# A third seven-product pair, wider operations and alternating PSUM banks in a decoder block's up/gate product

## The chip, the cores and the metric

The kernel runs on 1 core of a Trainium2 chip. The metric is the device time of one execution in microseconds (us). The five engines of the core are called here TensorE (PE in the profile; its weight loads are PEld), VectorE (DVE), ScalarE (ACT), GpSimd (POOL) and SyncE (SP, which issues nearly all DMA transfers here). Matmul results go to PSUM, which has eight banks of 512 float32 columns; everything else lies in SBUF.

## The reference

One decoder block on 256 rows of width 2048, in float32: two attention mixers, a gated sum, LayerNorm, a SwiGLU layer and LayerNorm again. The part that matters here is the SwiGLU layer, whose hidden width is 5632:

```python
def _swiglu(h, w_ffn_in, w_ffn_out):
    g, u = jnp.split(h @ w_ffn_in, 2, axis=-1)
    return (jax.nn.silu(g) * u) @ w_ffn_out
```

`h` is 256 x 2048, `w_ffn_in` 2048 x 11264 and `w_ffn_out` 5632 x 2048.

## The kernel before

Every product is computed to nearly float32 with the fp32r matmul: a value is split into a high part (ScalarE casts it, L71) and a low part (VectorE subtracts the high part, L72), and each product is three matmuls, high x high, high x low and low x high (`mm3`, L91 to L93). A matmul takes a 128 x 128 stationary tile of activations and a 128 x 512 moving tile of weights.

The hidden width is cut into 11 blocks of 512 columns. Block 0 is a plain product. Blocks 1 to 10 run through `pair_product` (L708). Such a block has four results, gate and up for the two halves of the rows (c11, c12, c21, c22: `acc_fg0`, `acc_fu0`, `acc_fg1`, `acc_fu1`), each in a PSUM bank of the tag `acc`. It takes the 16 slices of the inner dimension two at a time: eight pairs, each with one load of 1 MB (four tiles of 512 columns, `raw_fp`). An ordinary pair needs eight products, 24 matmuls. Pairs 2 and 4 (the third and the fifth) of blocks 1 to 9 use a Strassen-like form with seven products, 21 matmuls: VectorE combines the four weight tiles with four adds and subtractions of 512 columns (L737 to L740, in place in `raw_fp`), and ScalarE and VectorE split these combined tiles again. Four of the seven products (p1, p6, p7, p5) are shared among results; they add up over the seven-product pairs of a block in four banks of the tag `tmp`, and VectorE adds them into the results afterwards (L752 to L755, then L758 to L761). Matching forms of the activations are made once, in `row_forms` (L676), during block 0.

The splits work on halves of a load: 1024 columns, or 512 where only three tiles are needed. Names: `whfp_5g` is the high part of pair 5's gate half, `wlfp_5g` the low part, `whfp_4t` and `wlfp_4t` those of pair 4's combined tiles (t2, t3). High and low parts lie in two rings of eight buffers, the loads in a ring of three. After the results come silu and product (L774, L775, L787), a transpose of 32 x 32 blocks on VectorE (L264) into `rt`, and eight ticks later 16 transfers of 32 KB that SyncE issues (L286), which put `rt` into place in `act`.

The kernel is written in a tile framework whose list scheduler sets each engine's order at compile time, from the program's order and its own estimates; every engine then runs its instructions strictly in that order. The order in this part is thus not written by hand, and a change of sizes or buffers can move instructions.

Of the kernel before, what the change touches and what calls it, by code (L numbers as in the profile page):

```python
# [12 lines left out]
F32R = mybir.dt.float32r  # L13
# [4 lines left out]
P = 128  # L18
# [11 lines left out]
N = 512  # L30
# [14 lines left out]
def decoder_block(ctx, tc, xT, x, wz, lam_qk, subln, wa, wb, wo, g1, b1, b1T, wf, wfp, wfo, g2, b2,  # L45
# [9 lines left out]
    def bigt(shape, dt, name):  # L55
        return big.tile([P] + shape, dt, tag="big", name=name)
# [7 lines left out]
    def acc(name):  # L64
        return ps.tile([P, N], F32, tag="acc", name=name)

    def tmp(name):
        return ps.tile([P, N], F32, tag="tmp", name=name)

    def split(src, hi, lo, eng=None):  # L70
        nc.scalar.copy(hi, src)  # L71
        (eng or nc.vector).tensor_sub(lo, src, hi)  # L72


    def split_weights(part, name, eng=None):
        wh = wp.tile([P, 2, N], F32R, tag="wh", name="wh" + name)
        wl = wp.tile([P, 2, N], F32R, tag="wl", name="wl" + name)
        split(part.rearrange("p (a n) -> p a n", n=N), wh, wl, eng)
        return wh, wl

    def weights(src, name, loads=1, pool=()):
        raw = wp.tile([P, 2048], F32, tag="raw", name="raw_" + name, bufs=3)
# [88 lines left out]
    def weights_and_x(src, name):  # L171
        c = int(name.split("_")[-1])
        for i in range(2):
            k0 = 4 * c + 2 * i
            raw = wp.tile([P, 2, N], F32, tag="raw", name="raw%d_%s" % (i, name), bufs=3)
            sv = src[:, i * 1024:(i + 1) * 1024].rearrange("p (a n) -> p a n", n=N)
            if k0 == 0:
                wh = wp.tile([P, 2, N], F32R, tag="wh", name="whf")
                wl = wp.tile([P, 2, N], F32R, tag="wl", name="wlf")
                xss = []  # L180
                for a in range(2):
                    xss.append(x_part(a, 1))
                    nc.sync.dma_start(raw[:, a, :], sv[:, a, :])
                for a in range(2):
                    split_x(xss[a], a, 1)
                    split(raw[:, a, :], wh[:, a, :], wl[:, a, :])
                yield wh, wl
            else:
                xs = x_part(k0, 2)
                nc.sync.dma_start(raw, sv)  # L190
                split_x(xs, k0, 2)
                yield split_weights(raw.rearrange("p a n -> p (a n)"), "%d_%s" % (i, name))
# [477 lines left out]

    SEVEN = (2, 4)
    forms = []

    def row_forms():  # L676
        ns = len(SEVEN)
        full = bigt([NM, 2 * ns, P], F32, "hfull")
        fs = bigt([4, ns, P], F32, "forms")
        hl = bigt([2, 4, ns, P], F32R, "formshl")  # L680
        for m in range(NM):
            for n, i in enumerate(SEVEN):
                nc.vector.tensor_add(full[:, m, 2 * n:2 * n + 2, :], hth[m][:, 2 * i:2 * i + 2, :], htl[m][:, 2 * i:2 * i + 2, :])
        a = [[full[:, m].rearrange("p (n t) q -> p n t q", t=2)[:, :, t, :] for t in range(2)] for m in range(NM)]
        nc.vector.tensor_add(fs[:, 0], a[1][0], a[1][1])
        nc.vector.tensor_sub(fs[:, 1], fs[:, 0], a[0][0])
        nc.vector.tensor_sub(fs[:, 2], a[0][0], a[1][0])
        nc.vector.tensor_sub(fs[:, 3], a[0][1], fs[:, 1])
        split(fs, hl[:, 0], hl[:, 1])
        forms.append(hl)  # L690

    def stat_s(f, n):
        return forms[0][:, 0, f - 1, n, :], forms[0][:, 1, f - 1, n, :]

    def load_pair(j, i):
        raw = wp.tile([P, 4, N], F32, tag="raw", name="raw_fp%d_%d" % (j, i), bufs=3)
# [2 lines left out]

    def halves(src, name):  # L700
        n = src.shape[1]
        wh = wp.tile([P, 2, N], F32R, tag="wh", name="wh" + name)
        wl = wp.tile([P, 2, N], F32R, tag="wl", name="wl" + name)
        split(src, wh[:, 0:n], wl[:, 0:n])
        return [(wh[:, a, :], wl[:, a, :]) for a in range(n)]


    def pair_product(j):  # L708
        nk = KD // 2
        seven = SEVEN if j < NB_F - 1 else ()  # L710
        c11, c12, c21, c22 = [acc("acc_f%s_%d" % (c, j)) for c in ("g0", "u0", "g1", "u1")]
        ps_ = {}
        for i in range(nk):
            nm = "fp%d_%d" % (j, i)
            raw = load_pair(j, i)
            k0, k1 = 2 * i, 2 * i + 1
            first, final = i == 0, i == nk - 1
            if i not in seven:
                b11, b21 = halves(raw[:, 0:2], nm + "g")
                b22, b12 = halves(raw[:, 2:4], nm + "u")  # L720
                for ac, m, w0, w1 in ((c11, 0, b11, b21), (c12, 0, b12, b22), (c21, 1, b11, b21), (c22, 1, b12, b22)):
                    mm3(ac, *stat_h(m, k0), *w0, first, False)
                    mm3(ac, *stat_h(m, k1), *w1, False, final)
                tick()
                tick()
                continue
            n = seven.index(i)
            s0, s1 = n == 0, n == len(seven) - 1
            if s0:
                for f in (1, 6, 7, 5):  # L730
                    ps_[f] = tmp("p%d_%d" % (f, j))
            b11, b21 = halves(raw[:, 0:2], nm + "g")
            b22, = halves(raw[:, 2:3], nm + "u")
            mm3(ps_[1], *stat_h(0, k0), *b11, s0, s1)
            mm3(c11, *stat_h(0, k1), *b21, False, False)
            mm3(c12, *stat_s(4, n), *b22, False, False)
            nc.vector.tensor_sub(raw[:, 2], raw[:, 2], raw[:, 3])  # L737
            nc.vector.tensor_sub(raw[:, 3], raw[:, 3], raw[:, 0])
            nc.vector.tensor_add(raw[:, 0], raw[:, 2], raw[:, 0])
            nc.vector.tensor_sub(raw[:, 1], raw[:, 1], raw[:, 0])  # L740
            t2, t4 = halves(raw[:, 0:2], nm + "t2")
            t3, t1 = halves(raw[:, 2:4], nm + "t3")
            tick()
            mm3(ps_[6], *stat_s(2, n), *t2, s0, s1)
            mm3(ps_[7], *stat_s(3, n), *t3, s0, s1)
            mm3(ps_[5], *stat_s(1, n), *t1, s0, s1)
            mm3(c21, *stat_h(1, k1), *t4, False, False)
            tick()
            if s1:
                p1, u2, u3, t = [scr("%s_%d" % (c, j)) for c in ("p1", "u2", "u3", "u4")]  # L750
                nc.scalar.copy(p1, ps_[1])
                nc.vector.tensor_add(u3, p1, ps_[6])  # L752
                nc.vector.tensor_add(u2, u3, ps_[7])
                nc.vector.tensor_add(u3, u3, ps_[5])
                nc.vector.tensor_add(t, u2, ps_[5])  # L755
        if not seven:
            return (c11, c12), (c21, c22)
        nc.vector.tensor_add(p1, p1, c11)  # L758
        nc.vector.tensor_add(u3, u3, c12)
        nc.vector.tensor_add(u2, u2, c21)  # L760
        nc.vector.tensor_add(t, t, c22)  # L761
        return (p1, u3), (u2, t)
# [125 lines left out]
    with tc.manual_schedule():  # L888
# [26 lines left out]
        j = NB_D - 1  # L915
# [74 lines left out]
```

## Time and profile before

| | us |
|---|---|
| median of 3 runs | 1380.2 |
| lowest, highest | 1379.7, 1380.85 |
| profiled execution, own time | 1384.1 |
| its span in the trace | 1382.3 |
| TensorE busy in the span | 1365.0 (99%) |
| VectorE busy | 916.9 (66%) |
| ScalarE busy | 644.5 (47%) |

A share of busy time is an average over stages with different limits. What a change in one stage is worth is read from that stage: what each engine does there from one block to the next, and what ends its waits. The blocks 1 to 10 run from 705.26 to 1132.22 us of the span.

### The profile page before, as it was taken

Reading aid. Unit: us, or ns where it says so; the run is one execution under the profiler, and the core shown is the slowest. Engines: PE = TensorE matmul, PEld = TensorE weight load, DVE = VectorE, ACT = ScalarE, POOL = GpSimd, SP = SyncE. Lnnn points to the kernel's source line nnn. Section 1 sums busy time; section 2 is a strip of 40 time slices with the busy share of each in tenths; the row PEclk is TensorE's granted clock in tenths of the full one; section 3 lists DMA queues with packets and bytes.
Section 4 is the critical chain, followed back from the end, with each engine's and each line's share of the span. In section 5 each row is a group of like instructions: output and inputs, shape, how many; then the busy total and the mean of one; then the engine's idle time right before and its main releaser. Section 6 shows DMA issues by size and latency. Waiting matters only on the chain.

```text
span 1382.3 us, 16276 instructions
## 1 busy us (share of the span) xinstructions
PE 1365.0 (99%) x6110; PEld 1126.0 (81%) x6110; DVE 916.9 (66%) x1161; ACT 644.5 (47%) x866; POOL 57.2 (4%) x64
## 2 busy tenths in 40 slices
PE   8999999999999999999999999999999999999997
PEld 6888888888888888888888888888788788888886
DVE  6666566766645454575878888888787765554555
ACT  4463444546444434443644455445454444444441
POOL 0001010100000000100000000000000000000003
PEclk9999999999999999999999999999999999999999
DMA  8583645464454649663445664546745676555541
GB/s 281 192 302 145 223 166 198 179 217 152 156 225 162 249 138 356 221 244 122 161 161 192 248 244 182 195 171 247 254 170 195 230 280 225 206 186 191 205 152 61
DMA packets 57151, 279.45 MB, mean 202 GB/s; under 512 B 10224, under 2 KB 22640, under 8 KB 25712
## 3 DMA queue, kind: packets, MB, share of 16 engines
q1 hardware_dynamic: 56784, 278.08, 55.2%
q8 instruction: 48, 0.79, 0.2%
q10 hardware_dynamic: 288, 0.33, 0.1%
q14 instruction: 31, 0.25, 0.1%
HBM read 264.74 MB, written 2.10 MB: 193 GB/s over the span
## 4 chain that ended last, share of the span: by engine, by line
PE 79%; DVE 9%; DMA 7%; ACT 2%; issue 2%; SPq 1%; POOL 0%; POOLq 0%; ACTq 0%; DVEq 0%
PE oacc L91 6%; PE oacc L93 6%; PE oacc L92 6%; DMA raw_fp<-in_wfp 5%; PE acc_fu L91 3%; PE acc_fu L93 3%; PE acc_fu L92 3%; PE acc_fg L91 3%; PE acc_fg L93 3%; PE acc_fg L92 3%; PE acc_gA L91 2%; PE acc_gB L93 2%; PE acc_gA L93 2%; PE acc_gA L92 2%; PE acc_gB L92 2%; PE acc_gB L91 2%
## 5 line engine op out<-in xcount | busy, mean ns | idle before, releaser
L72 DVE TENSOR_TENSOR wl_fo<-raw_fo,wh_fo 128x1024 fp32r<-128x1024 f32 x84 | 102.5, 1225 | 98.5 <-ACT wh_fo L71 93.4
L71 ACT CAST wh_fo<-raw_fo 128x1024 fp32r<-128x1024 f32 x84 | 88.2, 1055 | 115.4 <-PE oacc L93 99.2
L93 PE MATMUL oacc<-wh_fo,ahl 128*128 128x512 f32 x332 | 129.3, 389 | 0.0
L91 PE MATMUL oacc<-wh_fo,ahl 128*128 128x512 f32 x332 | 129.2, 389 | 0.0
L92 PE MATMUL oacc<-wl_fo,ahl 128*128 128x512 f32 x332 | 129.2, 389 | 0.0
L93 PEld LDWEIGHTS oacc<-wh_fo,ahl 128*128 128x128 f32 x332 | 62.3, 188 | 13.4 <-DVE ahl L72 0.3
L91 PEld LDWEIGHTS oacc<-wh_fo,ahl 128*128 128x128 f32 x332 | 62.3, 188 | 12.9
L92 PEld LDWEIGHTS oacc<-wl_fo,ahl 128*128 128x128 f32 x332 | 62.3, 188 | 12.9
L72 DVE TENSOR_TENSOR wl_gA<-raw_gA,wh_gA 128x1024 fp32r<-128x1024 f32 x32 | 38.9, 1220 | 35.9 <-ACT wh_gA L71 35.7
L72 DVE TENSOR_TENSOR wl_o<-raw_o,wh_o 128x1024 fp32r<-128x1024 f32 x32 | 39.5, 1235 | 33.9 <-ACT wh_o L71 33.9
L71 ACT CAST wh_gA<-raw_gA 128x1024 fp32r<-128x1024 f32 x32 | 33.6, 1054 | 53.3 <-PE acc_brB L93 20.0
L71 ACT CAST wh_o<-raw_o 128x1024 fp32r<-128x1024 f32 x32 | 33.7, 1054 | 48.5 <-PE acc_o L93 33.9
L72 DVE TENSOR_TENSOR wl_gB<-raw_gB,wh_gB 128x1024 fp32r<-128x1024 f32 x32 | 38.6, 1222 | 19.9 <-ACT wh_gB L71 19.3
L91 PE MATMUL acc_o<-wh_o,mth 128*128 128x512 f32 x128 | 50.4, 394 | 0.0
L91 PE MATMUL acc_gA<-wh_gA,xth 128*128 128x512 f32 x128 | 50.2, 392 | 0.0
L91 PE MATMUL acc_gB<-wh_gB,xth 128*128 128x512 f32 x128 | 50.1, 391 | 0.0
L93 PE MATMUL acc_o<-wh_o,mtl 128*128 128x512 f32 x128 | 49.9, 390 | 0.0
L92 PE MATMUL acc_o<-wl_o,mth 128*128 128x512 f32 x128 | 49.8, 389 | 0.0
L93 PE MATMUL acc_gB<-wh_gB,xtl 128*128 128x512 f32 x128 | 49.8, 389 | 0.0
L92 PE MATMUL acc_gA<-wl_gA,xth 128*128 128x512 f32 x128 | 49.8, 389 | 0.0
L92 PE MATMUL acc_gB<-wl_gB,xth 128*128 128x512 f32 x128 | 49.8, 389 | 0.0
L93 PE MATMUL acc_gA<-wh_gA,xtl 128*128 128x512 f32 x128 | 49.8, 389 | 0.0
(515 smaller groups left out, 3761.9 us busy)
## 6 DMA issues: line engine op xcount, KB each, us to landing
raw_fp<-in_wfp SPq DMA_DIRECT2D x80, 1024.0 KB, 5.9
raw_fo<-in_wfo SPq DMA_DIRECT2D x44, 1024.0 KB, 4.8
raw_gA<-in_wz SPq DMA_DIRECT2D x16, 1024.0 KB, 4.9
raw_gB<-in_wz SPq DMA_DIRECT2D x16, 1024.0 KB, 5.0
raw_o<-in_wo SPq DMA_DIRECT2D x16, 1024.0 KB, 4.8
raw_vA<-in_wz SPq DMA_DIRECT2D x8, 1024.0 KB, 5.1
raw_qB<-in_wz SPq DMA_DIRECT2D x8, 1024.0 KB, 6.9
raw_kB<-in_wz SPq DMA_DIRECT2D x8, 1024.0 KB, 5.2
```

The lines of the kernel that those rows point to most:

```text
L71: nc.scalar.copy(hi, src)
L72: (eng or nc.vector).tensor_sub(lo, src, hi)
L91: nc.tensor.matmul(ac, xh, wh, start=start, stop=False)
L92: nc.tensor.matmul(ac, xh, wl, start=False, stop=False)
L93: nc.tensor.matmul(ac, xl, wh, start=False, stop=stop)
```

## The change

Four edits, all but the first in the up/gate product:

- `split_weights` (used by all other products) puts high and low parts into one tile of a ring of eight, in place of two tiles of two rings. The operations on them keep their sizes.
- `halves` splits a whole load of 2048 columns with one cast and one subtraction (1536 where three tiles are needed). In a seven-product pair the split of the combined tiles is also one operation of 2048 columns on each engine.
- `SEVEN` has a third entry: pair 6 too is computed with seven products, so `row_forms` makes three forms in place of two.
- In blocks with an even number the results take the banks of the tag `tmp` and the shared products those of `acc`; in odd blocks it is as before.

```diff
-        wh = wp.tile([P, 2, N], F32R, tag="wh", name="wh" + name)
-        wl = wp.tile([P, 2, N], F32R, tag="wl", name="wl" + name)
-        split(part.rearrange("p (a n) -> p a n", n=N), wh, wl, eng)
-        return wh, wl
+        w = wp.tile([P, 4, N], F32R, tag="w", name="w" + name)
+        split(part.rearrange("p (a n) -> p a n", n=N), w[:, 0:2], w[:, 2:4], eng)
+        return w[:, 0:2], w[:, 2:4]
...
-    SEVEN = (2, 4)
+    SEVEN = (2, 4, 6)
...
-        hl = bigt([2, 4, ns, P], F32R, "formshl")
+        hl = bigt([2, 4, 2, P], F32R, "formshl")
+        more = [[sp.tile([P, 4, P], F32R, tag="s", name="forms%d_%d" % (n, k)) for k in range(2)] for n in range(2, ns)]
...
-        split(fs, hl[:, 0], hl[:, 1])
-        forms.append(hl)
+        split(fs[:, :, 0:2], hl[:, 0], hl[:, 1])
+        for n in range(2):
+            forms.append([hl[:, k, :, n] for k in range(2)])
+        for n, hi_lo in enumerate(more):
+            split(fs[:, :, 2 + n], *hi_lo)
+            forms.append(hi_lo)
...
     def halves(src, name):
         n = src.shape[1]
-        wh = wp.tile([P, 2, N], F32R, tag="wh", name="wh" + name)
-        wl = wp.tile([P, 2, N], F32R, tag="wl", name="wl" + name)
+        wh = wp.tile([P, 4, N], F32R, tag="w", name="wh" + name)
+        wl = wp.tile([P, 4, N], F32R, tag="w", name="wl" + name)
         split(src, wh[:, 0:n], wl[:, 0:n])
...
-        c11, c12, c21, c22 = [acc("acc_f%s_%d" % (c, j)) for c in ("g0", "u0", "g1", "u1")]
+        acc_c, acc_p = (acc, tmp) if j % 2 else (tmp, acc)
+        c11, c12, c21, c22 = [acc_c("acc_f%s_%d" % (c, j)) for c in ("g0", "u0", "g1", "u1")]
...
-                b11, b21 = halves(raw[:, 0:2], nm + "g")
-                b22, b12 = halves(raw[:, 2:4], nm + "u")
+                b11, b21, b22, b12 = halves(raw, nm)
...
-                    ps_[f] = tmp("p%d_%d" % (f, j))
-            b11, b21 = halves(raw[:, 0:2], nm + "g")
-            b22, = halves(raw[:, 2:3], nm + "u")
+                    ps_[f] = acc_p("p%d_%d" % (f, j))
+            b11, b21, b22 = halves(raw[:, 0:3], nm)
...
-            t2, t4 = halves(raw[:, 0:2], nm + "t2")
-            t3, t1 = halves(raw[:, 2:4], nm + "t3")
+            t2, t4, t3, t1 = halves(raw, nm + "t")
```

The lines behind the edits move by up to five: the combining adds are L742 to L745 in the changed kernel, the shared adds L756 to L759, the result adds L762 to L765, the silu products L779 and L791, the transposes L263, the loads L702 and the transfers L285.

Three places show what the scheduler makes of it. First VectorE in pair 4 of block 5, before:

```order
L72 TENSOR_TENSOR wlfp5_4g_7025<-raw_fp5_4_7022,whfp5_4g_7024 128x1024
L72 TENSOR_TENSOR wlfp5_4u_7029<-raw_fp5_4_7022,whfp5_4u_7028 128x512
L737 TENSOR_TENSOR raw_fp5_4_7022<-raw_fp5_4_7022 128x512
L738 TENSOR_TENSOR raw_fp5_4_7022<-raw_fp5_4_7022 128x512
L739 TENSOR_TENSOR raw_fp5_4_7022<-raw_fp5_4_7022 128x512
L740 TENSOR_TENSOR raw_fp5_4_7022<-raw_fp5_4_7022 128x512
L72 TENSOR_TENSOR wlfp5_4t2_7046<-raw_fp5_4_7022,whfp5_4t2_7045 128x1024
L72 TENSOR_TENSOR wlfp5_4t3_7050<-raw_fp5_4_7022,whfp5_4t3_7049 128x1024
```

Now VectorE in the same block's pair 6, which had two subtractions of 1024 columns, up to the first shared add:

```order
L72 TENSOR_TENSOR wlfp5_6_6700<-raw_fp5_6_6697,whfp5_6_6699 128x1536
L742 TENSOR_TENSOR raw_fp5_6_6697<-raw_fp5_6_6697 128x512
L743 TENSOR_TENSOR raw_fp5_6_6697<-raw_fp5_6_6697 128x512
L744 TENSOR_TENSOR raw_fp5_6_6697<-raw_fp5_6_6697 128x512
L745 TENSOR_TENSOR raw_fp5_6_6697<-raw_fp5_6_6697 128x512
L72 TENSOR_TENSOR wlfp5_6t_6717<-raw_fp5_6_6697,whfp5_6t_6716 128x2048
L72 TENSOR_TENSOR wlfp5_7_6744<-raw_fp5_7_6741,whfp5_7_6743 128x2048
L756 TENSOR_TENSOR u3_5_6734<-p1_5_6732,p6_5_6550 128x512
```

Pairs 2 and 4 have the same six rows; nothing stands between the last combining add and the subtraction that waits for the cast of its result.

Second, VectorE at a block's end, before: the next block's pairs 0, 1 and the first part of pair 2 stand ahead of the result adds.

```order
L72 TENSOR_TENSOR wlfp4_0g_6522<-raw_fp4_0_6519,whfp4_0g_6521 128x1024
L72 TENSOR_TENSOR wlfp4_0u_6526<-raw_fp4_0_6519,whfp4_0u_6525 128x1024
L72 TENSOR_TENSOR wlfp4_1g_6556<-raw_fp4_1_6553,whfp4_1g_6555 128x1024
L72 TENSOR_TENSOR wlfp4_1u_6560<-raw_fp4_1_6553,whfp4_1u_6559 128x1024
L72 TENSOR_TENSOR wlfp4_2g_6594<-raw_fp4_2_6587,whfp4_2g_6593 128x1024
L72 TENSOR_TENSOR wlfp4_2u_6598<-raw_fp4_2_6587,whfp4_2u_6597 128x512
L758 TENSOR_TENSOR p1_3_6388<-p1_3_6388,acc_fg0_3_6176 128x512
```

Now, at the same place on VectorE, between blocks 3 and 4:

```order
L72 TENSOR_TENSOR wlfp4_0_6187<-raw_fp4_0_6184,whfp4_0_6186 128x2048
L757 TENSOR_TENSOR u2_3_6126<-u3_3_6127,p7_3_5944 128x512
L762 TENSOR_TENSOR p1_3_6125<-p1_3_6125,acc_fg0_3_5876 128x512
...
L765 TENSOR_TENSOR u4_3_6128<-u4_3_6128,acc_fu1_3_5879 128x512
...
L263 STREAM_TRANSPOSE rt3_6174<-sl3_1_6171 128x4x4x32
L72 TENSOR_TENSOR wlfp4_1_6217<-raw_fp4_1_6214,whfp4_1_6216 128x2048
```

Pair 1 and pair 2 have moved behind the block's whole tail.

Third, SyncE in block 4 before, where the 16 transfers belong to block 3 (`rt3`):

```order
L697 DMA raw_fp4_3_6634<-in_wfp 128x2048
L697 DMA raw_fp4_4_6684<-in_wfp 128x2048
L286 DMA act1_5837<-rt3_6509 32x256 x16
L697 DMA raw_fp4_5_6736<-in_wfp 128x2048
L697 DMA raw_fp4_6_6770<-in_wfp 128x2048
```

And now:

```order
L702 DMA raw_fp4_3_6283<-in_wfp 128x2048
L285 DMA act1_5572<-rt3_6174 32x256 x16
L702 DMA raw_fp4_4_6329<-in_wfp 128x2048
L702 DMA raw_fp4_5_6364<-in_wfp 128x2048
L702 DMA raw_fp4_6_6394<-in_wfp 128x2048
```

The transfers have moved ahead of pair 4's load in blocks 2 to 10. In block 1 they stand behind it, as before.

## Rows read from the trace of the kernel before

**Rows 1.** Page, part 1: busy us, share of span, instructions of an engine.

```profile
PE 1365.0 (99%) x6110; PEld 1126.0 (81%) x6110; DVE 916.9 (66%) x1161; ACT 644.5 (47%) x866; POOL 57.2 (4%) x64
```

**Rows 2.** Busy time of each engine in blocks 2, 7, 8, 9, 10.

```profile
core 0: us, PE busy (x) PEld busy (x) DVE busy (x) ACT busy (x) POOL busy (x), PEclk, DMA share, GB/s
...
747.42:789.58 42.16, 42.16 (x188) 34.91 (x186) 35.18 (x42) 20.85 (x23) 0.00 (x0) 1.00 0.57 212
...
958.22:1001.89 43.67, 42.32 (x187) 34.75 (x186) 34.91 (x41) 20.18 (x23) 0.00 (x0) 1.00 0.60 210
1001.89:1044.83 42.94, 42.69 (x187) 34.76 (x187) 35.73 (x43) 20.68 (x24) 0.00 (x0) 1.00 0.54 208
1044.83:1088.24 43.41, 42.64 (x186) 34.76 (x187) 35.12 (x42) 21.10 (x24) 0.00 (x0) 1.00 0.62 224
1088.24:1132.22 43.98, 43.85 (x192) 36.03 (x193) 27.89 (x30) 19.23 (x23) 0.00 (x0) 1.00 0.60 223
```

**Rows 3.** Timeline of TensorE (start, length, instruction, [idle before]): blocks 1, 8, output product.

```profile
705.26 0.39 PE L91 MATMUL acc_fg<-whfp_0g,hth 128*128 128x512 f32 x1
...
1001.89 0.47 PE L91 MATMUL acc_fg<-whfp_0g,hth 128*128 128x512 f32 x1 [1.35 <-DVE p L758]
...
1132.22 0.40 PE L91 MATMUL oacc<-wh_fo,ahl 128*128 128x512 f32 x1
```

**Rows 4.** Timeline of VectorE, blocks 5 and 6.

```profile
911.50 1.23 DVE L72 TENSOR_TENSOR wlfp_2g<-raw_fp,whfp_2g 128x1024 fp32r<-128x1024 f32 x1 [1.47 <-ACT whfp_2g L71]
...
917.44 0.68 DVE L761 TENSOR_TENSOR u<-u,acc_fu 128x512 f32<-128x512 f32 x1
918.04 0.69 DVE L775 TENSOR_TENSOR sl<-sl,u 128x512 f32<-128x512 f32 x1
...
920.44 0.70 DVE L264 STREAM_TRANSPOSE rt<-sl 128x512 f32<-128x512 f32 x1
...
925.19 1.22 DVE L72 TENSOR_TENSOR wlfp_3g<-raw_fp,whfp_3g 128x1024 fp32r<-128x1024 f32 x1
926.33 1.22 DVE L72 TENSOR_TENSOR wlfp_3u<-raw_fp,whfp_3u 128x1024 fp32r<-128x1024 f32 x1
...
928.60 0.69 DVE L72 TENSOR_TENSOR wlfp_4u<-raw_fp,whfp_4u 128x512 fp32r<-128x512 f32 x1
929.32 0.69 DVE L737 TENSOR_TENSOR raw_fp<-raw_fp 128x512 f32<-128x512 f32 x1
...
931.50 0.69 DVE L740 TENSOR_TENSOR raw_fp<-raw_fp 128x512 f32<-128x512 f32 x1
933.38 2.36 DVE L72 TENSOR_TENSOR wlfp_4t<-raw_fp,whfp_4t 128x1024 fp32r<-128x1024 f32 x2 [1.20 <-ACT whfp_4t L71]
938.82 1.23 DVE L72 TENSOR_TENSOR wlfp_5g<-raw_fp,whfp_5g 128x1024 fp32r<-128x1024 f32 x1 [3.08 <-ACT whfp_5g L71]
...
954.57 1.23 DVE L72 TENSOR_TENSOR wlfp_2g<-raw_fp,whfp_2g 128x1024 fp32r<-128x1024 f32 x1 [1.53 <-ACT whfp_2g L71]
```

**Rows 5.** Timeline of ScalarE: casts in blocks 5 and 6.

```profile
894.46 1.05 ACT L71 CAST whfp_5g<-raw_fp 128x1024 fp32r<-128x1024 f32 x1 [2.19 <-DMA raw_fp<-in_wfp]
...
911.37 0.62 ACT L71 CAST whfp_2u<-raw_fp 128x512 fp32r<-128x512 f32 x1
...
937.74 1.05 ACT L71 CAST whfp_5g<-raw_fp 128x1024 fp32r<-128x1024 f32 x1 [3.44 <-DMA raw_fp<-in_wfp]
```

**Rows 6.** SyncE's queue (start, time until all are issued, count), blocks 5 and 6.

```profile
879.15 10.01 SPq L286 DMA_DIRECT2D act<-rt  x16
889.26 1.00 SPq L697 DMA_DIRECT2D raw_fp<-in_wfp  x2
921.17 11.03 SPq L286 DMA_DIRECT2D act<-rt  x16
932.30 1.00 SPq L697 DMA_DIRECT2D raw_fp<-in_wfp  x2
```

**Rows 7.** Page, part 6: loads of the up/gate weights, count, size, median us to landing.

```profile
raw_fp<-in_wfp SPq DMA_DIRECT2D x80, 1024.0 KB, 5.9
```

More of the change, by code (lines that the diff above doesn't have):

```diff
@@ L177, in weights_and_x @@
             if k0 == 0:
-                wh = wp.tile([P, 2, N], F32R, tag="wh", name="whf")
-                wl = wp.tile([P, 2, N], F32R, tag="wl", name="wlf")
+                w = wp.tile([P, 4, N], F32R, tag="w", name="wf")
+                wh, wl = w[:, 0:2], w[:, 2:4]
                 xss = []
@@ L688, in row_forms @@
         nc.vector.tensor_sub(fs[:, 3], a[0][1], fs[:, 1])
-        split(fs, hl[:, 0], hl[:, 1])
-        forms.append(hl)
+        split(fs[:, :, 0:2], hl[:, 0], hl[:, 1])
[4 more added lines that the diff above has]
+            forms.append(hi_lo)
     def stat_s(f, n):
-        return forms[0][:, 0, f - 1, n, :], forms[0][:, 1, f - 1, n, :]
+        return tuple(t[:, f - 1, :] for t in forms[n])
     def load_pair(j, i):
```

## The prediction

> **What bounds the kernel now.** I read the page first, then the busy time cut at the starts of the up/gate blocks, then single instructions. The page has TensorE busy for 1365.0 of 1382.3 us [rows 1]: the program is TensorE's, and only the blocks 1 to 10 of the up/gate product are touched. A block of 186 matmuls takes 42.16 us at granted clock 1.00, that is 0.2267 us a matmul, with no gap inside [rows 2, 3]. The stretches of blocks 7, 8 and 9 are longer by 1.51, 0.78 and 1.25 us, and the last block (192 matmuls, 43.52 us) by 0.46 [rows 2]: 4.0 us in which TensorE waits for VectorE to read the result banks (L758) before it writes them again [rows 3].
>
> VectorE is busy for some 35 of 42.16 us of such a block [rows 2]. Its order is fixed, so its waits must be added. In the block from 916 us on it idles 1.20 us, twice, for a cast of combined weights, which cannot start before the four combining adds end, and 3.08 us for the cast of pair 5 [rows 4]. That one is SyncE's doing: pair 5's load stands behind the 16 transfers of the turned block, which SyncE issues from 921.17 to 932.30, and lands 5.4 us later [rows 5, 6]. From pair 2's first subtraction to the next block's it takes 43.1 us (911.50 to 954.57) [rows 4]: VectorE's loop with its waits is already as long as TensorE's, and its lead is used up when the waits at L758 appear. So I price the change on VectorE's loop.
>
> **The change part by part.** *TensorE.* Nine blocks lose three matmuls each: 27 x 0.2267 = 6.1 us, and a block needs 183 x 0.2267 = 41.5 us. The banks that change sides can remove the 4.0 us at most. The three extra forms cost VectorE about 2 us before block 1 (the four 128x1024 ops of this kind take 1.2 us each [rows 4]); TensorE works on block 0 then, from prepared weights, so nothing.
>
> The Trainium skill ("Perfetto Trace Analysis", Optimizing Tensor Performance, Matmuls) says that independent matmul groups should rotate through banks so that one group's evacuation overlaps the next group's matmuls. The trace agrees with a wait of that kind; by that rule alone the change would give its 4.0 us.
>
> *Wider operations.* On VectorE 512 columns go start to start in 0.60 us, 1024 in 1.14 [rows 4]; so a column costs 1.05 ns and an operation 0.07 us, and 1536 and 2048 columns take 1.67 and 2.20 us. Eleven merges a block save 0.7 us. On ScalarE 512 columns last 0.62 us and 1024 1.05 [rows 5], so 1536 last 1.48 and 2048 1.91. A subtraction must now wait for the whole cast. From the last combining add's start to the subtraction's start it is 1.88 us with a cast of 1.05 in it (931.50 to 933.38) [rows 4]; with 1.91 it is 2.74, and VectorE's idle time in it grows from 1.2 to 2.0 us, three times a block.
>
> The Trainium skill (same page, Optimizing Scalar/DVE Operations) has larger operations raise the throughput of a saturated engine, but smaller ones finish earlier where an unsaturated engine makes others wait. By the first the merge is worth its 0.7 us, by the second it costs the longer waits; the rows have both, and the second is larger here.
>
> *The third seven-product pair.* An eight-product pair costs VectorE 2.20 us now. A seven-product pair costs 1.67 for the first subtraction, 0.12 more until its dependent follows, three adds 0.73 apart (929.32 to 931.50) [rows 4] and the 2.74, in sum 6.71 us, and 2.20 for the second subtraction: 8.91. The exchange is worth +6.7 us of VectorE's loop against 0.68 us of TensorE.
>
> *The order.* Two moves follow from it. At a block's end VectorE has prepared only pair 0 of the next block when it takes the tail (it had 0, 1 and half of 2 before), so the tail's waits are no longer covered. And the 16 transfers now stand ahead of pair 4's load on SyncE, where they stood ahead of pair 5's; pairs 5, 6, 7 and the next block's loads queue behind both.
>
> Now one period of VectorE, from the start of the add of the last result bank (L761 before, L765 now). That add, four silu products and the first transpose at 0.60 each, and 0.70 for the second transpose: 4.3 us. SyncE follows 0.03 later [rows 4, 6]; the 16 transfers keep it 10.1 us in one block and 11.1 in another [rows 6], I take 10.6; from pair 4's issue to its cast 5.20 and 5.44 us [rows 5, 6], 5.3; cast 1.48 + 0.03. So pair 4's subtraction starts at 21.8. (VectorE itself would be ready at 4.3 + 2.2 + 8.9 + 2.2 = 17.6; it loses 4.2 there.) From there: 6.71 + 2.20 for pair 4, 2.20 for pair 5, 6.71 + 2.20 for pair 6, 0.13 because ScalarE copies a shared product, 512 columns, before pair 7's cast, 2.20 for pair 7, 0.60 for the first shared add, 2.20 for the next block's pair 0, and six adds at 0.60 until the last result bank again: 28.75. **Period 50.5 us.** TensorE is ready before that: it has pair 7's low part at about 44 us and needs 22 more matmuls, 5 us, so its last bank is full at about 49. The same reckoning in the block from 916 us on, with its own values (3.7 + 0.03 + 11.13 + 5.44 + 1.08), puts pair 5's subtraction 21.4 us behind L761; it is 938.82 - 917.44 = 21.4 [rows 4].
>
> **The sum.** Block 1 still has its lead: pair 4's load precedes the transfers there, every subtraction ends before TensorE asks for it, and the block takes 41.5 us, from 705.26 [rows 3] to 746.8. Its tail add then starts at 747.0. Eight periods (blocks 2 to 9; the first is 0.6 shorter, since one product precedes the add) bring that add to 747.0 + 8 x 50.5 - 0.6 = 1150.4. The last block has only eight-product pairs; its pair 4 is late the same way: 4.3 + 10.6 + 5.3 + 1.9 + 2.3 = 24.4 us after the add, then 22 matmuls and 3 x 5.44 us, so it ends 46 us after it, at 1196.4, where it ended at 1132.2 [rows 3]. That is **+64 us**. The output product behind it keeps its order and its length. The profiled run took 1384.1 us (span 1382.3), so 1448 in its terms; the median of 1380.2 is 3.9 below it, which leaves **1445 us**.
>
> Errors of this sum: the transfers at 10.1 or 11.1 move a period by 0.5 either way, a landing after 5.2 or 5.9 us (the median of all these loads [rows 7]) by -0.1 or +0.6. Operations of 2048 columns have no row; stretched from 1024 they may be off by 0.1 us each, 1 us a period. So a period lies between 48.9 and 52.6, and eight of them with the last block's share give a range of 1432 to 1462 for this case.
>
> **The rivals.**
> - *Pair 4's load isn't late.* If the transfers took SyncE less, or the loop without them were what counts, VectorE's own chain is the bound: 39.9 us of work and three waits of 2.0, 45.9 us a period. That gives 747.0 + 8 x 45.9 - 0.6 = 1113.6 and a last block of 43.7: +25, **1405 us**. Against it: SyncE's rows show pair 5's load leaving only after the sixteenth transfer [rows 6]. 0.11.
> - *TensorE stays the bound*, and VectorE hides all of its new work. Then the whole 6.1 + 4.0 comes off: **1370 us**, faster. It decides if VectorE's loop stays under 41.5 us, so at work plus waits of 45.9 some 4.4 us of my rows would have to be wrong, and the late load absent too. For it: TensorE is the engine at 99%. Against it: the loop of 43.1 us that VectorE has already. 0.05. Half-way between this and the first rival it would look like no change: 0.02.
> - *TensorE's clock falls.* TensorE now idles 9 us a block, in pieces of 1 to 3 us. In the trace its longest wait in these blocks is 1.35 us, and the granted clock stays at 1.00, the 2.4 GHz level, in that stretch [rows 2, 3]; a longer one isn't there. If the 12 matmuls behind each of five waits ran at half speed, 5 x 12 x 0.2267 = 13.6 us against 9 of slack: +4.6 a block, +37, **1482 us**. 0.07.
>
> The Trainium skill ("TensorE: Matmul & The Clock Gate", What's actually happening) has an idle TensorE fall to the 1.2 GHz level and return after sustained work; that is this last rival's mechanism. No run here shows the lower level yet.
>
> **How the numbers follow.** The forecast has 0.75, the rivals 0.11, 0.05, 0.02 and 0.07. The likeliest time is 1445. From 1404 to 1462 lies the forecast's range and the first rival; left out are TensorE's bound, the fallen clock, and the forecast's own tail, together under 0.2. Faster by over 0.2% (about what a measurement of this kernel can tell) 0.05, within it 0.02, slower 0.93.
>
> **What would show it.** In the changed profile: blocks 2 to 9 some 50 us apart, not 42; TensorE's matmuls waiting for the low parts written by VectorE in pairs 1, 2, 4 and 6, and no wait for result banks; VectorE idle about 2 us before each combined subtraction, and about 4 before pair 4's first one, released by ScalarE and that by the load; pair 4's load issued right behind the 16 transfers; 183 matmuls at 0.2267 us a block. Wrong would be blocks of 41.5 us (VectorE's work is hidden after all), blocks of 46 (the load is not what binds), or a granted clock below 0.95 in 750 to 1150 us.

## The result and the profile after

The changed kernel takes 1449.8 us (median of 4 runs, 1443.4 to 1451.1); the kernel before, run beside it, 1380.5. The ratio is 1.049, with a 95% interval of 1.046 to 1.052: slower by 69 us. The profiled execution shown here took 1449.8 us, its span 1448.0.

The page of the changed kernel, busy time of each engine and the up/gate loads (answers to [rows 1, 7]):

```profile
PE 1389.0 (96%) x6083; PEld 1126.8 (78%) x6083; DVE 952.8 (66%) x1111; ACT 643.2 (44%) x778; POOL 57.4 (4%) x64
...
raw_fp<-in_wfp SPq DMA_DIRECT2D x80, 1024.0 KB, 5.2
```

TensorE has 27 matmuls less (6.1 us), yet it is busy 24 us longer, and its share fell from 99% to 96%. About half of these 30 us are slow matmuls: 72 of those in the blocks start while the granted clock is at its lower level (more on this below) and take some 0.21 us more each, 15 us. The other half is how waits look in this number: a matmul beside a wait is drawn 0.39 to 0.50 us long, where matmuls in a stream start 0.2267 us apart. With the transfers on GpSimd (below), at a granted clock of 1.00 in these blocks, the same 6083 matmuls are still busy for 1372.1 us. One period of the up/gate product, from tail add to tail add (L765, 898.92 to 949.62), as VectorE's timeline shows it (start, length, instruction, [idle time before, and what ended it]):

```profile
898.92 0.68 DVE L765 TENSOR_TENSOR u<-u,acc_fu 128x512 f32<-128x512 f32 x1
...
901.92 1.30 DVE L263 STREAM_TRANSPOSE rt<-sl 128x512 f32<-128x512 f32 x2
...
912.02 2.29 DVE L72 TENSOR_TENSOR wlfp_2t<-raw_fp,whfp_2t 128x2048 fp32r<-128x2048 f32 x1 [2.05 <-ACT whfp_2t L71]
914.23 2.28 DVE L72 TENSOR_TENSOR wlfp<-raw_fp,whfp 128x2048 fp32r<-128x2048 f32 x1
920.37 1.76 DVE L72 TENSOR_TENSOR wlfp<-raw_fp,whfp 128x1536 fp32r<-128x1536 f32 x1 [3.85 <-ACT whfp L71]
922.16 0.69 DVE L742 TENSOR_TENSOR raw_fp<-raw_fp 128x512 f32<-128x512 f32 x1
...
924.34 0.69 DVE L745 TENSOR_TENSOR raw_fp<-raw_fp 128x512 f32<-128x512 f32 x1
927.07 2.29 DVE L72 TENSOR_TENSOR wlfp_4t<-raw_fp,whfp_4t 128x2048 fp32r<-128x2048 f32 x1 [2.04 <-ACT whfp_4t L71]
929.28 3.95 DVE L72 TENSOR_TENSOR wlfp<-raw_fp,whfp 128x2048 fp32r<-128x2048 f32 x2
...
938.19 2.29 DVE L72 TENSOR_TENSOR wlfp_6t<-raw_fp,whfp_6t 128x2048 fp32r<-128x2048 f32 x1 [2.06 <-ACT whfp_6t L71]
941.03 2.29 DVE L72 TENSOR_TENSOR wlfp<-raw_fp,whfp 128x2048 fp32r<-128x2048 f32 x1 [0.54 <-ACT whfp L71]
...
949.62 0.68 DVE L765 TENSOR_TENSOR u<-u,acc_fu 128x512 f32<-128x512 f32 x1
```

ScalarE's cast behind the long wait, and SyncE's queue (start, time until all are issued, count) in the same block; beside [rows 4 to 6], where pair 5 is the late one:

```profile
918.86 1.48 ACT L71 CAST whfp<-raw_fp 128x1536 fp32r<-128x1536 f32 x1 [5.06 <-DMA raw_fp<-in_wfp]
...
938.59 0.59 ACT L755 COPY p<-p 128x512 f32<-128x512 f32 x1 [0.43 <-PE p L92]
```

```profile
903.25 10.02 SPq L285 DMA_DIRECT2D act<-rt  x16
913.38 16.34 SPq L702 DMA_DIRECT2D raw_fp<-in_wfp  x4
```

VectorE waits for nothing but ScalarE in this period, five times: about 2.05 us for each of the three combined casts, 3.85 us for the cast of pair 4, and 0.54 us for the cast of pair 7. Before pair 4's cast ScalarE itself waited for that pair's load. That load left SyncE at 913.38, right behind the sixteen transfers. The nine L765 stand at 746.37, 797.07, 848.97 and so on to 1152.17: eight periods of 49.9 to 51.9 us, mean 50.7, where a block took 42.16 [rows 2]. The output product starts at 1198.0 (1132.22 before [rows 3]) and is as long as it was, 250.0 against 250.1 us, and block 1 starts no later (704.6 against 705.26): all of the loss lies in these blocks, and the first edit, on the splits of the other products, costs nothing that shows.

### The profile page after: what moved, and what is told of

Its sections match the earlier page's. It is cut to its first block, busy times and chain, and to the rows that moved or that the text cites. A ratio compares the mean times of both kernels' runs of the same rounds, so it can differ in the third digit from the quotient of the medians.

```text
span 1448.0 us, 15982 instructions
## 1 busy us (share of the span) xinstructions
PE 1389.0 (96%) x6083; PEld 1126.8 (78%) x6083; DVE 952.8 (66%) x1111; ACT 643.2 (44%) x778; POOL 57.4 (4%) x64
## 4 chain that ended last, share of the span: by engine, by line
PE 77%; DVE 10%; ACT 5%; DMA 4%; issue 3%; SPq 1%; POOL 0%; ACTq 0%; POOLq 0%; DVEq 0%
PE oacc L92 5%; PE oacc L90 5%; PE oacc L91 5%; DVE wlfp L72 4%; DMA raw_fp<-in_wfp 3%; ACT whfp L71 3%; PE acc_fg L91 3%; PE acc_fg L92 2%; PE acc_fu L91 2%; PE acc_fg L90 2%; PE acc_fu L90 2%; PE acc_fu L92 2%; PE acc_gA L90 2%; PE acc_gB L92 2%; PE acc_gA L92 2%
## 5 line engine op out<-in xcount | busy, mean ns | idle before, releaser
L72 DVE TENSOR_TENSOR wlfp<-raw_fp,whfp 128x1536 fp32r<-128x1536 f32 (+1 forms) x80 | 166.6, 2103 | 55.3 <-ACT whfp L71 49.9
L71 ACT CAST whfp<-raw_fp 128x1536 fp32r<-128x1536 f32 (+1 forms) x80 | 139.2, 1761 | 98.8 <-DMA raw_fp<-in_wfp 83.8
L72 DVE TENSOR_TENSOR w_fo<-raw_fo,w_fo 128x1024 fp32r<-128x1024 f32 x84 | 102.2, 1224 | 95.2 <-ACT w_fo L71 90.5
L71 ACT CAST w_fo<-raw_fo 128x1024 fp32r<-128x1024 f32 x84 | 87.9, 1054 | 112.5 <-PE oacc L92 97.3
L90 PE MATMUL oacc<-w_fo,ahl 128*128 128x512 f32 x332 | 129.2, 389 | 0.0
L91 PE MATMUL oacc<-w_fo,ahl 128*128 128x512 f32 x332 | 129.2, 389 | 0.0
L92 PE MATMUL oacc<-w_fo,ahl 128*128 128x512 f32 x332 | 129.0, 389 | 0.0
L90 PE MATMUL acc_fg<-whfp,hth 128*128 128x512 f32 x239 | 97.8, 409 | 9.5 <-ACT whfp L71 9.4
L91 PE MATMUL acc_fg<-wlfp,hth 128*128 128x512 f32 x239 | 94.5, 395 | 9.7 <-DVE wlfp L72 9.7
L92 PE MATMUL acc_fg<-whfp,htl 128*128 128x512 f32 x239 | 93.3, 390 | 0.0
L90 PE MATMUL acc_fu<-whfp,hth 128*128 128x512 f32 x212 | 84.7, 400 | 0.0
L91 PEld LDWEIGHTS oacc<-w_fo,ahl 128*128 128x128 f32 x332 | 62.3, 188 | 13.1
L92 PEld LDWEIGHTS oacc<-w_fo,ahl 128*128 128x128 f32 x332 | 62.2, 188 | 13.1 <-DVE ahl L72 0.2
L90 PEld LDWEIGHTS oacc<-w_fo,ahl 128*128 128x128 f32 x332 | 62.3, 188 | 12.8
```

Source lines behind the costliest of these rows:

```text
L90: nc.tensor.matmul(ac, xh, wh, start=start, stop=False)
L91: nc.tensor.matmul(ac, xh, wl, start=False, stop=False)
L92: nc.tensor.matmul(ac, xl, wh, start=False, stop=stop)
```

## Experiments

The theory: VectorE's chain sets the period. Its parts are its work (three seven-product pairs), the waits for combined casts of 2048 columns, and the late load of pair 4. The rivals: the load only looks late; VectorE's work would be hidden; TensorE's clock, or its banks, carry the loss.

### Is it the late load? Transfers by GpSimd, or two ticks later

```diff
-                nc.sync.dma_start(dst[32 * b:32 * b + 32, i], rt[32 * i:32 * i + 32, b])
+                nc.gpsimd.dma_start(dst[32 * b:32 * b + 32, i], rt[32 * i:32 * i + 32, b])
```

> The changed kernel with one edit: the 16 transfers of a turned block into act are issued by GpSimd instead of SyncE. Every engine keeps its order; SyncE only loses these transfers, so no load stands behind them. The theory (pair 4's load, late behind the 16 transfers, sets the period of 50.7 us): the load leaves early, VectorE no longer waits about 4 us for pair 4's cast, and its own chain of 45.9 us a block (39.9 of work and three waits of 2.0) is what is left, so blocks 2 to 9 stand 46 us apart and the time falls from 1449.8 by 8 x 4.8 and some 2 in the last block, to about 1409 (1402 to 1417). The rival (TensorE's fallen clock, or VectorE's chain itself, is what sets the period, and the load only looks late): blocks still 50 to 51 us apart, 1443 to 1450. A second rival (VectorE's work is hidden once the load is on time): blocks of 41.5 us, about 1375.

Measured: 1413.6 us, ratio to before 1.023 (1.021 to 1.025). The periods are 46.2 us, seven times alike. The second run leaves the transfers with SyncE and changes only their place in its queue:

```diff
-        later(8, lambda j=j, rt=rt: move_blocks(...
+        later(10, lambda j=j, rt=rt: move_blocks(...
```

> The changed kernel with one number changed: the 16 transfers of a turned block are due 10 ticks after the block in place of 8. VectorE and ScalarE keep their order in blocks 3 to 10; on SyncE 5 of the transfers stand ahead of pair 4's load and 11 behind it, ahead of pair 5's. All stay on SyncE. The theory (what costs the 4.5 us a period between the changed kernel and the kernel with transfers on GpSimd is only that pair 4's load stands behind all 16): 11 transfers of 0.63 us less bring pair 4's load 6.9 us earlier, which is more than VectorE's wait of 3.85 us there; pair 5's load is issued some 14 us behind the tail add and is there, cast, at 22, before VectorE comes to it at 26. So no load is late, the blocks stand 46.2 us apart, 1410 to 1416. The rival (SyncE's transfers delay loads or casts wherever they stand, or GpSimd's issue changed something else): 1430 to 1450.

Measured: 1412.1 us, ratio 1.022 (1.019 to 1.024), periods of 46.22 us. SyncE's queue in it, and VectorE's tail adds and only waits in that period:

```profile
890.79 3.05 SPq L285 DMA_DIRECT2D act<-rt  x5
893.95 0.52 SPq L702 DMA_DIRECT2D raw_fp<-in_wfp  x1
894.51 6.99 SPq L285 DMA_DIRECT2D act<-rt  x11
901.88 27.65 SPq L702 DMA_DIRECT2D raw_fp<-in_wfp  x7
```

```profile
886.46 0.68 DVE L765 TENSOR_TENSOR u<-u,acc_fu 128x512 f32<-128x512 f32 x1
...
899.56 2.29 DVE L72 TENSOR_TENSOR wlfp_2t<-raw_fp,whfp_2t 128x2048 fp32r<-128x2048 f32 x1 [2.05 <-ACT whfp_2t L71]
...
910.68 2.29 DVE L72 TENSOR_TENSOR wlfp_4t<-raw_fp,whfp_4t 128x2048 fp32r<-128x2048 f32 x1 [2.05 <-ACT whfp_4t L71]
...
921.80 2.29 DVE L72 TENSOR_TENSOR wlfp_6t<-raw_fp,whfp_6t 128x2048 fp32r<-128x2048 f32 x1 [2.06 <-ACT whfp_6t L71]
...
932.68 0.68 DVE L765 TENSOR_TENSOR u<-u,acc_fu 128x512 f32<-128x512 f32 x1
```

The wait of 3.85 us is gone, the three waits for combined casts stay, and the period is 40.1 us of work and 6.2 of waits. Two different ways of letting pair 4's load go earlier give the same time within 1.5 us, so it is the place in the queue and nothing that GpSimd does. (The 1.5 us lie behind the blocks: with transfers by GpSimd the output product takes 251.9 us in place of 250.0, in this run and in the three later ones that have them there.) The late load costs 36 to 38 us of the 69. What is left is VectorE's own chain, at the period that the prediction gave its first rival (45.9).

### Is it the third pair? Undone, and alone

```diff
-    SEVEN = (2, 4, 6)
+    SEVEN = (2, 4)
```

> The changed kernel with the third seven-product pair undone (pairs 2 and 4 as before); 2048 columns and changing banks stay. In the order, pairs 0, 1 and the first part of pair 2 of the next block stand ahead of the tail on VectorE again, and the 16 transfers ahead of pair 5's load. The theory (the third pair's 6.7 us of VectorE and the order it brings are the loss): VectorE's chain is some 39 to 40 us a block, under TensorE's 42.16, pair 5's load is late by about 1 us at most, so blocks of 42.2 to 43.2 us and 1376 to 1386, no slower than the kernel before by more than 0.5%. The rival (the wide operations with their longer waits are the loss by themselves): blocks of 45 us or more, over 1400.

Measured: 1380.4 us, ratio 0.999 (0.998 to 1.000). TensorE is busy in every microsecond from 705 to 1125. So 2048 columns and changing banks cost nothing that can be measured as long as VectorE has its lead. The other way round, the third pair in the kernel before (splits of 1024 and 512 columns, banks fixed):

```diff
-                b11, b21, b22, b12 = halves(raw, nm)
+                b11, b21 = halves(raw[:, 0:2], nm + "g")
+                b22, b12 = halves(raw[:, 2:4], nm + "u")
...
-        acc_c, acc_p = (acc, tmp) if j % 2 else (tmp, acc)
+        acc_c, acc_p = (acc, tmp)
```

(and likewise for the other two splits; high and low part of a half share one tile)

> The kernel before with the third seven-product pair alone: all splits at 1024 or 512 columns as before, banks fixed. In the order VectorE now takes the whole tail, transposes too, ahead of pair 0 of the next block; on SyncE 5 transfers stand ahead of pair 3's load and 11 ahead of pair 4's. The theory (it is VectorE's added work and the lost lead that cost): VectorE's work with its waits is 5 x 2.28 for the ordinary pairs, 3 x 8.2 for the others and 8.5 for sums, silu and transposes, 44.5 us; TensorE cannot go on at a block's start until VectorE has done the tail, some 5 to 6 us on top of its 41.5; so a period of 45 to 48 us and 1404 to 1428. The rival (the third pair costs little by itself, and the wide operations make the loss): 1375 to 1390.

Measured: 1425.8 us, ratio 1.032 (1.030 to 1.034), periods of 47.2 to 48.8 us from block 3 on. TensorE's two costliest waits in seven periods (instruction, what it waits for: us in total, times, longest):

```profile
PE acc_fg L91 <- DVE whfp_0g L72: 12.6, 6, 2.2
PE p L90 <- ACT whfp_2g L71: 9.6, 6, 1.7
```

(Here one tile holds high and low parts, so `whfp_0g` written by DVE is the low part.) The first wait, for pair 0's low part, is the lost lead: VectorE takes the tail before pair 0. The expectation left out that pair 4's load is late here too, behind 11 transfers; VectorE and ScalarE in one of these periods:

```profile
955.07 1.22 DVE L72 TENSOR_TENSOR whfp_4g<-raw_fp,whfp_4g 128x1024 fp32r<-128x1024 f32 x1 [2.33 <-ACT whfp_4g L71]
```

```profile
953.99 1.05 ACT L71 CAST whfp_4g<-raw_fp 128x1024 fp32r<-128x1024 f32 x1 [3.06 <-DMA raw_fp<-in_wfp]
```

So the third pair alone costs 45 us, with the order that it brings, a late load in it and a granted clock of 0.986 over the run. The wide operations add 24, with another move of the transfers (now all ahead of pair 4's load), where they cost nothing without the third pair. The edits are not additive: a wait costs only where its engine is the bound.

### Is it the width? Combined tiles at 1024 columns

```diff
-        split(src, wh[:, 0:n], wl[:, 0:n])
+        for c in ((slice(0, 2), slice(2, 4)) if name.endswith("t") else (slice(0, n),)):
+            split(src[:, c], wh[:, c], wl[:, c])
```

> The changed kernel with one width undone: the combined tiles of a seven-product pair are split in two casts and two subtractions of 1024 columns, all else stays at 2048, with three seven-product pairs and changing banks. The order on the engines is otherwise the same in blocks 3 to 10. The theory (VectorE's chain from pair 4's subtraction on lies wholly on the path): each combined wait falls by 0.86 us and the two subtractions cost 0.08 more; pairs 4 and 6 lie behind the late load, so a period loses 1.6 us and eight of them 12.5: about 1437 (1433 to 1441), VectorE's idle time before the first combined subtraction 1.2 us. The rival (TensorE, not VectorE's chain, ends last in a period): within 2 us of 1449.8.

Measured: 1419.0 us, ratio 1.027 (1.025 to 1.029), 31 us under the changed kernel where 12.5 were expected. The periods of blocks 3 to 9 are 2.9 us shorter (47.9 against 50.7), not 1.6. Pair 4 in that kernel, VectorE and ScalarE (line numbers are one higher):

```profile
908.71 0.69 DVE L745 TENSOR_TENSOR raw_fp<-raw_fp 128x512 f32<-128x512 f32 x1
909.44 0.69 DVE L746 TENSOR_TENSOR raw_fp<-raw_fp 128x512 f32<-128x512 f32 x1
910.05 2.42 DVE L72 TENSOR_TENSOR wlfp_4t<-raw_fp,whfp_4t 128x1024 fp32r<-128x1024 f32 x2
913.06 3.96 DVE L72 TENSOR_TENSOR wlfp<-raw_fp,whfp 128x2048 fp32r<-128x2048 f32 x2 [0.59 <-ACT whfp L71]
```

```profile
908.79 1.05 ACT L71 CAST whfp_4t<-raw_fp 128x1024 fp32r<-128x1024 f32 x1 [3.35 <-DVE raw_fp L744]
910.16 1.05 ACT L71 CAST whfp_4t<-raw_fp 128x1024 fp32r<-128x1024 f32 x1 [0.33 <-DVE raw_fp L746]
```

The expectation carried the 1.2 us wait of [rows 4] over. Here the first cast starts after the second combining add (L744), not after the fourth, beside the other two adds, and the wait is gone altogether; 0.59 us comes back at pair 5's cast. That is 1.3 us for a combined pair. The rest was the order: in block 2 the transfers stand behind pair 4's load, and its period is 41.8 us, not 50.7, which is another 8.9. So this run shows the direction of the width and the size of a split wait, but its 31 us are the width's and the order's together.

### Do the banks matter? Alone, and undone

The kernel before with changing banks alone:

> The kernel before with one edit: in blocks with an even number results and shared products change banks. No engine's order changes. The theory of the prediction has two readings. If the waits for result banks are all that the banks cost, the 4.0 us of TensorE's waits in blocks 7 to 10 go: 1376.5, faster by 0.3%. If VectorE's loop of 43.1 us a block is itself the limit in those blocks, TensorE waits for a low part instead, as long as before: 1380 to 1381, no change. It can't be slower by more than 0.2% by either.

Measured: 1379.75 us, ratio 0.998 (0.997 to 0.999). TensorE waits for nothing in blocks 1 to 10, and every seven-product block takes 42.16 us: the ten blocks last 422.97 us, 3.99 less than before (704.56 to 1127.53, against 705.26 to 1132.22 [rows 3]). The first reading was right in the trace, and the time agrees with it, 1 to 4 us by its interval. In the changed kernel without changing banks:

> The changed kernel with the changing of banks undone: results in the banks of the one tag and shared products in the other in every block. No engine's order changes in blocks 3 to 10. The theory (VectorE's chain sets the period, and TensorE has over 1 us of slack in it): TensorE waits for the result adds at each block's start, some 1 to 2 us, and the time stays within 4 us of 1449.8. The rival (the change of banks carries a part of the period, since VectorE's last adds also wait for TensorE): 1455 to 1470.

Measured: 1448.8 us, ratio 1.049 (1.046 to 1.051), periods of 49.7 to 52.4 us. Off the path, as the theory has it; but the wait of 1 to 2 us that I expected at each block's start isn't there at all. VectorE takes the first result add (L762, at 946.23 in this run) 3 us before the last (L765, at 949.22); since no wait for it is among TensorE's, the first bank is read before TensorE comes back to it.

### Is VectorE's chain all of it? Taking work and waits off it

Transfers by GpSimd, combined tiles at 1024 columns, and besides:

```diff
-            nc.vector.tensor_mul(ts_[m], ts_[m], ups[m])
+            (nc.gpsimd if 0 < j < NB_F - 1 else nc.vector).tensor_mul(ts_[m], ts_[m], ups[m])
```

> The changed kernel with three edits that take work and waits off VectorE: transfers by GpSimd, combined tiles split at 1024 columns, and the two products of silu and up half made by GpSimd in blocks 1 to 9 (1.3 us each in the trace of the kernel before). Three seven-product pairs and changing banks stay. The theory (the loss is only VectorE's chain; its 46.2 us with timely loads fall by 1.3 each in pairs 2 and 4 and 1.5 in pair 6 by the other runs, and by 1.2 for the two products, to 40.9): TensorE's 183 matmuls at 0.2267, 41.5 us, bind again, nine blocks are 0.68 us shorter than with two pairs, and the time is 1379.8 - 6.1 = 1374 (1372 to 1378). The rival (VectorE's chain stays a little above 41.5, through slower operations beside GpSimd's or a wait for its products): blocks of 42 to 43.5 us, 1379 to 1392.

Measured: 1385.4 us, ratio 1.003 (1.002 to 1.004), periods of 41.8 to 43.0 us. The rival held. VectorE and GpSimd at the ends of two blocks:

```profile
877.81 2.84 DVE L72 TENSOR_TENSOR wlfp<-raw_fp,whfp 128x1536 fp32r<-128x1536 f32 x1
880.58 0.70 DVE L263 STREAM_TRANSPOSE rt<-sl 128x512 f32<-128x512 f32 x1
881.84 0.71 DVE L263 STREAM_TRANSPOSE rt<-sl 128x512 f32<-128x512 f32 x1 [0.56 <-POOL sl L792]
...
919.97 2.28 DVE L72 TENSOR_TENSOR wlfp<-raw_fp,whfp 128x2048 fp32r<-128x2048 f32 x1
```

```profile
877.44 4.36 POOL L792 TENSOR_TENSOR sl<-sl,u 128x512 f32<-128x512 f32 x2 [29.73 <-DVE sl L780]
...
916.84 1.29 POOL L792 TENSOR_TENSOR sl<-sl,u 128x512 f32<-128x512 f32 x1 [26.14 <-DVE sl L780]
920.19 3.20 POOL L792 TENSOR_TENSOR sl<-sl,u 128x512 f32<-128x512 f32 x1 [2.06 <-DVE sl L780]
```

The subtraction that lasts 1.76 us in the changed kernel lasts 2.84 here, and two products of 1.3 us last 4.36. It adds up if they take turns: the first product ends about 878.7, then the subtraction runs some 1.8 us to 880.6, then the second product 1.3 us to 881.8. At the next block's end the product beside VectorE's result adds takes 1.29 us, and the one that starts 0.2 us behind a subtraction of 2.28 us takes 3.20. So VectorE gained nothing by giving the products away: it saved two operations of 0.60 us, lost 1.08 us in the longer subtraction, and its transposes now wait for GpSimd. The Trainium skill ("SBUF — State Buffer", SBUF: two separate sides) has such a VectorE operation with two SBUF inputs and a GpSimd operation exclude each other; these rows agree, 2.84 against 1.76 us.

Now without GpSimd's products, but with 1024 columns also in pairs 3, 5 and 7, whose casts ended the remaining waits of 0.6 us:

```diff
-        split(src, wh[:, 0:n], wl[:, 0:n])
+        for c in ((slice(0, 2), slice(2, 4)) if name[-1] in "t357" else (slice(0, n),)):
+            split(src[:, c], wh[:, c], wl[:, c])
```

> The changed kernel with transfers by GpSimd, and with casts and subtractions of 1024 columns just where VectorE waited for ScalarE: for the combined tiles, and for pairs 3, 5 and 7, which follow them. All other splits stay at 1536 and 2048; three seven-product pairs and changing banks stay; GpSimd makes no products. The theory (the loss is VectorE's chain alone): by the rows of the runs so far the chain is 3 x 6.87 for the seven-product pairs, 3 x 2.28 and 2 x 2.20 for the others, 4.8 for the sums, 2.4 for the products, 1.3 for the transposes, together 40.3 us without a wait, under TensorE's 41.5. So blocks of 41.5 us and 1379.8 - 6.1 = 1373.7 (1372 to 1377), faster than the kernel before by 0.5%. The rival (a wait not in that sum, at a block's start, where pair 2's combined tiles come close behind the tail, holds a block at 42 to 43): 1378 to 1388.

Measured: 1375.4 us, ratio 0.995 (0.994 to 0.996): faster than the kernel before by half a per cent, little but outside the interval. The same with pairs 3, 4 and 6 in place of 2, 4 and 6:

> As the run with narrow splits where VectorE waited, but the seven-product pairs are 3, 4 and 6 in place of 2, 4 and 6 (so the ordinary pairs behind them, split at 1024 columns, are 5 and 7). VectorE's work is 0.1 us less, and TensorE has three ordinary pairs, 16.3 us, before it needs combined tiles. The theory: TensorE is bound, blocks of 41.5 us, 1373.7 (1372 to 1377). If a wait at the block's start holds the other run above 1378, this one is free of it and comes out at 1374. The rival (two seven-product pairs in a row, 13.7 us of VectorE against 9.5 of TensorE, use up the lead): blocks above 42 us, 1378 to 1388.

Measured: 1376.2 us, ratio 0.995 (0.994 to 0.997). TensorE in blocks 1 to 9, in the first of the two (columns as in [rows 2]):

```profile
705.00:1125.00 420.00, 420.00 (x1855) 347.78 (x1854) 385.42 (x410) 215.17 (x201) 78.39 (x160) 1.00 0.60 219
```

No gap, and the last five periods are 41.5 us in both. With VectorE's chain under TensorE's 41.5 the third pair gives its 0.68 us a block. VectorE is busier here, 40.2 of a period's 41.48 us against 39.75 of 50.70 in the changed kernel; what went is its waits. The scheduler's order changed as well: VectorE now takes pair 1's subtraction ahead of the last three result adds, where in the changed kernel it stands behind the whole tail. These two runs thus show that the waits can go and that TensorE then binds; they don't divide the gain between transfers, widths and order, and narrow operations with the transfers on SyncE, two ticks later, were not run. So a VectorE that is hidden, the prediction's second rival, was there to be had, but not with this order and these widths.

## Why the prediction was right

Forecast 1445, measured 1449.8; the steps in their order.

- *VectorE's loop is the thing to price, and pair 4's load is late.* Right, and shown twice: with the load on time the periods fall from 50.7 to 46.2, the forecast's two figures being 50.5 and 45.9. The 43.1 us given for the loop of before were one block's; over all eight its tail adds (L761) stand 42.9 us apart, 747.91 to 1090.95, TensorE's own waits included.
- *The period.* To pair 4's subtraction 21.45 us, forecast 21.8: transfers 10.13 and not 10.6 (903.25 to 913.38), from the load's issue to its cast 5.48 and not 5.3. From there to the next L765 29.25, forecast 28.75. The half microsecond is one term: the copy of a shared product ahead of pair 7's cast was put at 0.13 us, and VectorE loses 0.63 there (0.54 of it shown as idle), because the copy itself waits 0.43 us for TensorE. That wait is 0 to 1.9 us from block to block (below). The two errors nearly cancel, which is luck.
- *2048 columns.* They had no row and were stretched from 1024: 2.20 us start to start, 1.91 for the cast, 2.0 for the wait; the rows show 2.21, 1.91 and 2.05.
- *Third pair against width.* The forecast spoke of both as terms of one sum. Right in the sum; but the third pair alone is 45 us, the widths alone are nothing that can be measured, and together they are 69. The sentence that by the Trainium skill's advice on larger operations ("Perfetto Trace Analysis", Optimizing Scalar/DVE Operations) the merge is worth its 0.7 us or costs the waits has this answer: without the third pair neither shows in the time (1380.4); with it the waits cost more, since cutting the combined splits in two took 2.9 us off a period.
- *Banks worth at most 4.0 us.* Right: alone 3.99 in the trace and 1 to 4 in the time, nothing in the changed kernel.
- *Block 1 and the last block.* First L765 at 746.4 (747.0), last block's end at 1198.0 (1196.4).
- *From the trace's terms to the median.* Here a step failed. The sum's 1448 in terms of the profiled run met that run's 1449.8 within 2 us; then I took off the 3.9 us by which the profiled run of before exceeded its median. The changed kernel's profiled run lies at its median. A profiled run's distance from the median is that one run's, and doesn't carry over; 3.9 of the 4.8 us missing are this. The distance may well be the 4.0 us of bank waits themselves: outside the blocks the trace of before is as long as that of the kernel with changing banks alone (705.26 and 250.1 us against 704.56 and 250.1), whose run took 1379.4 us. Then it lay inside the stretch that the sum replaces, and the 1370 of the second rival counted it twice: the last two kernels above, with three pairs and no gap in the blocks, take 1375 and 1376 (1.9 of it behind the blocks). Only one run of before was traced, so this isn't shown.
- *What TensorE waits for.* Partly wrong. I named low parts by VectorE, and two of the four rows are that; the longest wait by far is for the high part of pair 4's combined tiles, a cast by ScalarE. TensorE's waits in blocks 1 to 10 (us in total, times, longest):

```profile
PE p L90 <- ACT whfp_4t L71: 22.4, 8, 2.8
PE acc_fg L91 <- DVE wlfp L72: 9.7, 9, 1.7
PE acc_fg L90 <- ACT whfp L71: 9.4, 19, 0.6
PE p L91 <- DVE wlfp L72: 3.4, 5, 1.3
```

The cast waits for VectorE's adds, so the chain is the one described, one link earlier. No wait for result banks is among them, as said.

- *The fallen clock*, a rival at 0.07, does appear, and costs little. The block shown above, cut finely (columns as in [rows 2]), and then two whole periods:

```profile
925.00:928.00 3.00, 0.91 (x4) 0.67 (x4) 0.96 (x2) 2.86 (x2) 0.00 (x0) 1.00 0.00 0
928.00:930.00 2.00, 1.41 (x5) 0.91 (x4) 2.00 (x2) 2.00 (x2) 0.00 (x0) 0.61 0.00 0
930.00:932.00 2.00, 2.00 (x7) 1.58 (x6) 2.00 (x2) 0.21 (x1) 0.00 (x0) 0.53 0.67 188
932.00:935.00 3.00, 3.00 (x15) 2.47 (x14) 2.90 (x4) 0.00 (x0) 0.00 (x0) 1.00 1.02 429
```

(TensorE alone in these two: length, busy time, granted clock, DMA share, GB/s)

```profile
797.07:848.97 51.90, 46.48 (x185) 0.93 0.46 173
...
1051.23:1101.11 49.88, 44.77 (x185) 0.97 0.48 181
```

Behind the 2.8 us wait for pair 4's cast, matmuls follow each other 0.43 us apart (929.49, 929.92, 930.34) and not 0.2267, at a granted clock near 0.53, the 1.2 GHz level, and are back at 1.00 by 932. The rival had five waits a block do this, 12 matmuls each, and +4.6 us a period. In this kernel only the longest wait does it, for 7 or 8 matmuls in six blocks and 14 or 15 in two. Most of that is TensorE's slack; the rest seems to come out at ScalarE's copy of p1, which waits for TensorE:

```profile
837.95 0.59 ACT L755 COPY p<-p 128x512 f32<-128x512 f32 x1 [1.89 <-PE p L92]
...
1090.10 0.58 ACT L755 COPY p<-p 128x512 f32<-128x512 f32 x1
```

The period with the 1.89 us is the one at clock 0.93, the one without any wait lasts 49.9. The other block at 0.93 waits 1.16 us there, and those at 0.97 between 0 and 0.69; in sum it is 4.2 us over eight periods. So my estimate of the clock's part is some 4 us of the 69. The fastest of the four runs (1443.4) also has the highest mean granted clock, 0.992; the other three have 0.983 to 0.986, and among them the time doesn't follow it (1449.9 at 0.983, 1451.1 at 0.986). That the slow matmuls make the copy late is read off these eight blocks; no run takes the one away alone. With the load on time (both runs) the granted clock stays at 1.00 from 750 to 1100 us, so these 4 us are a part of the late load's 36 to 38. The Trainium skill ("TensorE: Matmul & The Clock Gate", What's actually happening) has an idle TensorE fall to 1.2 GHz and return after work; the trace agrees, 0.53 behind a wait of 2.8 us.

What stays open: why the sixteen transfers take 10.0 us in six of the eight blocks and 11.1 and 11.4 in two, as they did before in [rows 6].

## What to carry to other kernels

When TensorE is at 99%, add up the next engine's loop with its waits from the rows before giving that engine more work: a loop of 43.1 beside 42.16 us has no room for 6.7, whatever it saves elsewhere. Look at where the scheduler then puts small transfers in a queue of large loads; two ticks of delay were worth 38 us here. Use wide operations where the engine only works, and narrow ones where another engine waits for the first half: mixed that way, and with the transfers out of the loads' queue, the same change made the kernel 0.5% faster and not 4.9% slower.

## What the runs showed of the hardware that I had not expected

- The times of VectorE's subtraction and GpSimd's product, both on SBUF, add up as if they took turns: 2.84 us for 1.76 of work, 3.20 for a product of 1.29, and 4.36 for two.
- Sixteen transfers of 32 KB kept GpSimd's queue for 7.9 us (0.49 us each, where it didn't wait for one to land) and SyncE's for 10 to 11.4, and the loads on SyncE left beside GpSimd's.
- Each of the eight waits of 2.8 us went with a granted clock near 0.53 for 7 to 15 matmuls; where the longest wait from 750 to 1100 us was 1.03 us (transfers by GpSimd, or two ticks later) it stayed at 1.00. Between them the length of one wait doesn't decide: single waits of 1.2 and 1.7 us in the changed kernel's last block left the clock at 1.00, while with combined tiles at 1024 it fell behind waits of 1.63 and 1.29 us within 2 us of each other.
